# Who sums the weights of the down product, and when: accumulating transfers, VectorE and tile order in a decoder layer

## The chip, the cores and the metric

The kernel is one launch on one core of a Trainium2 chip. A core has TensorE (matrix products), VectorE, ScalarE and GpSimd (called PE, DVE, ACT and POOL in the profile) and SyncE (SP), which here only issues DMA transfers. Transfers issued by SP and by POOL go to the core's 16 DMA engines. A transfer issued by POOL can also add what it brings to what is at its destination (an accumulating transfer). Each engine works through its own instructions in order. The metric is the time of one execution in microseconds on the device; lower is better.

## The reference

One decoder layer on 512 tokens of width 1024, in float32: a gated linear recurrence and a sparse attention side by side, merged, and then a gated MLP with a short convolution. What bears on the change is the MLP's end:

```python
up = causal_dwconv(rms_norm(x, norm2_g) @ w_up, ffn_conv_w, ffn_conv_b)
gate, val = jnp.split(up, 2, axis=-1)
x = x + (jax.nn.gelu(gate) * val) @ w_down
```

`w_up` is 1024 x 6144 and `w_down` is 3072 x 1024.

## The kernel before

**Products.** A float32 product is made from three products of split operands: high times high, high times low, low times high (`mm3`, and `mm` in `down`, lines 1526 to 1528). So each weight tile is loaded raw, cast to a high part by ScalarE (`whi`, line 200), and VectorE or GpSimd subtracts to get the low part (`wlo`, lines 208 and 205).

**Strassen's scheme.** Most of the up product and all of the down product use the Strassen-Winograd form: a 2 x 2 block product from seven products instead of eight, for sums and differences of the blocks. The sums of weight blocks are needed as weight tiles of their own. For the up product and for part of the down product they are made in DRAM, long before they are needed: `sums` (lines 1254 to 1296) copies blocks to a DRAM tile (`ws6` to `ws23` for the up product, `dn0` to `dn11` for the down product) and adds others by accumulating transfers of POOL (line 1268). It has 83 steps. `_wprep` calls one or more of them as it prepares the weight tiles, whose order is `PLAN` (229 tiles; up product from index 97, the Strassen part from 109, down product from 181). `SUM_AT` is the index at which the first step is issued, `SUM_RATE` how far apart in tiles the next ones are, by index.

**The down product** (`down`, lines 1512 to 1621) has twelve tiles n of the inner dimension, each from two chunks of 128 rows. Phase one runs n = 0 to 11 with four of the seven products (tiles `d1` and `d2`, 1024 columns each), for four quarters p of the output columns, 48 matmuls for each n. Then `mix` combines the PSUM banks of each quarter with one copy on ScalarE and four additions on VectorE. Phase two runs n = 0 to 11 again with the other three products (`d3`, 1024 columns, and `d4`, 512), 36 matmuls for each n. `down_ops` and `down_ops2` make the activations' operands (`dt`, `dh`, `dl`) on VectorE and ScalarE.

**The loads.** `down_load(m)`, m = 0 to 23 over both phases, loads two raw tiles: `dg` and `ds`, from three slots each. In phase one `ds` becomes `d2`: its left half is a block of the weights, to which a second block has to be added; the right half comes from a DRAM sum. `dg` becomes `d1`: one block and another DRAM sum. Where n is odd or below 3, POOL adds the second block to `ds` by an accumulating transfer (line 1317). Elsewhere VectorE does, from `dg` (line 1333). In phase two the left half of `d3` is a DRAM sum plus one more block. For odd n that block is added in DRAM by an accumulating transfer in the load of phase one (line 1322). For even n VectorE adds it (line 1331).

**What sets the order.** On TensorE the order is as written. On the other engines a planner orders the instructions by its own cost estimates, by the order of the program and by priorities; `issue_after` puts an instruction behind a named one. `w` prepares weight tiles two ahead (`WLEAD`), and at the first tile of each n `_wprep` calls `down_load` two loads ahead and `down_sums` one tile ahead:

```python
if name in ("d1", "d3") and m:
    self.down_load(m + 2)
    self.down_sums(m + 1)
```

Phase two begins with tile 0 for quarters 0 to 2, then tile 1 for quarter 0, then tile 0 for quarter 3.

## Time and profile before

| what | value |
|---|---|
| median of 3 runs | 1040.7 us (1034.25 to 1041.61) |
| profiled execution | 1032.89 us |
| its span, first to last instruction | 1031.0 us |
| TensorE busy | 1006.5 us (98%) |
| VectorE busy | 810.3 us (79%) |
| ScalarE busy | 645.9 us (63%) |
| GpSimd busy | 275.1 us (27%) |
| moved by DMA | 186.66 MB, mean 181 GB/s |

The span is shorter than the execution, since it runs from the first to the last instruction. Busy time of TensorE is modelled and includes the pipelining of matmuls, so 98% doesn't mean that TensorE works at its peak in that time. A row of the timeline has the start and the length in us, the engine, the line, the operation and its tiles; in brackets stands how long the engine was idle before it and what ended the idle time. In the windows view each engine has its busy time and its number of instructions; then come the granted TensorE clock, the mean busy share of the 16 DMA engines and the GB/s they moved.

### The profile page before, as it was taken

To read this page: it belongs to the slowest core of one execution; us is meant where nothing else is said; L and a number is where in the kernel's file an instruction comes from. 1 tells how busy PE (TensorE), PEld (TensorE's weight loads), DVE (VectorE), ACT (ScalarE), POOL (GpSimd) and SP (SyncE) were. 2 spreads that over 40 slices of the span, in tenths; PEclk is the share of its full clock that TensorE was granted. 3 is DMA by queue.
4 is the path that set the end of the run, shared out by engine and by line. 5 is a ranking of instruction groups with operands and counts; after the bars stand their busy time and mean duration, and the time that the engine had idled before them with its cause. 6 is when DMAs were issued, how large, how long until landed. Compare 5 with 4: busy or idle time off the path is not lost.

```text
span 1031.0 us, 16984 instructions
## 1 busy us (share of the span) xinstructions
PE 1006.5 (98%) x6089; PEld 893.5 (87%) x6089; DVE 810.3 (79%) x1565; ACT 645.9 (63%) x1076; POOL 275.1 (27%) x353
## 2 busy tenths in 40 slices
PE   9998999999999999999999999999999999988998
PEld 7897888988888878888888888888999999987998
DVE  6778878889878778779598464599888888987876
ACT  6466776877777654488788543465566666654453
POOL 0166435335443320241332114222111111310000
PEclk9999999999999999999999999999999999999999
DMA  6537756677657797564534987655656566776553
GB/s 233 117 108 202 220 144 158 168 180 170 189 139 195 193 285 235 156 182 122 155 102 117 301 240 219 171 159 170 191 186 195 184 184 201 221 193 183 155 184 134
DMA packets 75365, 186.66 MB, mean 181 GB/s; under 512 B 18059, under 2 KB 19723, under 8 KB 71440
## 3 DMA queue, kind: packets, MB, share of 16 engines
q1 hardware_dynamic: 66064, 153.65, 45.6%
q0 software_dynamic: 9072, 31.77, 17.8%
q8 instruction: 48, 0.79, 0.3%
q14 instruction: 37, 0.30, 0.1%
q10 hardware_dynamic: 144, 0.15, 0.1%
HBM read 176.32 MB, written 58.20 MB: 227 GB/s over the span
## 4 chain that ended last, share of the span: by engine, by line
PE 71%; DVE 11%; DMA 10%; issue 3%; ACT 3%; POOL 1%; SPq 1%; DVEq 0%; ACTq 0%; POOLq 0%
PE mm L239 11%; PE mm L238 11%; PE mm L237 11%; PE mm L1417 6%; PE mm L1415 6%; PE mm L1416 6%; PE O L947 4%; DVE wlo L208 3%; PE T L956 3%; DMA wraw<-in_w 2%; PE mm L1527 2%; PE mm L1526 2%; PE mm L1528 2%; PE S L916 1%; PE S L917 1%
## 5 line engine op out<-in xcount | busy, mean ns | idle before, releaser
L200 ACT CAST whi<-wraw 128x1024 fp32r<-128x1024 f32 (+3 forms) x178 | 177.8, 999 | 135.5 <-PE mm L1416 56.4
L208 DVE TENSOR_TENSOR wlo<-wraw,whi 128x1024 fp32r<-128x1024 f32 (+2 forms) x145 | 166.2, 1146 | 56.3 <-ACT whi L200 56.2
L237 PE MATMUL mm<-xh,whi 128*128 128x512 f32 x456 | 178.7, 392 | 0.0
L239 PE MATMUL mm<-xh,wlo 128*128 128x512 f32 x456 | 178.5, 391 | 0.0
L238 PE MATMUL mm<-xl,whi 128*128 128x512 f32 x456 | 178.2, 391 | 0.0
L205 POOL TENSOR_TENSOR wlo<-wraw,whi 128x256 fp32r<-128x256 f32 (+1 forms) x131 | 96.8, 843 | 74.5 <-ACT whi L200 69.9
L239 PEld LDWEIGHTS mm<-xh,wlo 128*128 128x128 f32 x456 | 85.6, 188 | 18.4
L237 PEld LDWEIGHTS mm<-xh,whi 128*128 128x128 f32 x456 | 85.7, 188 | 16.9
L238 PEld LDWEIGHTS mm<-xl,whi 128*128 128x128 f32 x456 | 85.6, 188 | 16.9
L927 ACT ACTIVATE s<-s,bs,rq 128x128 f32<-128x128 f32 (+3 forms) x128 | 82.5, 647 | 19.1 <-DVE bs L924 19.0
L1528 PE MATMUL mm<-dh,wlo 128*128 128x256 f32 x300 | 85.1, 284 | 5.1 <-DVE wlo L208 5.1
L1527 PE MATMUL mm<-dl,whi 128*128 128x256 f32 x300 | 84.7, 282 | 3.8 <-DVE dl L263 3.8
L1526 PE MATMUL mm<-dh,whi 128*128 128x256 f32 x300 | 84.8, 283 | 0.1
L263 DVE TENSOR_TENSOR ptl<-T,pth 128x512 fp32r<-128x512 f32 x80 | 55.0, 688 | 17.3 <-ACT pth L262 16.4
L1268 POOL DMA_DIRECT2D ws<-ws x36 | 28.3, 786 | 136.0 <-DMA ws<-in_wa 68.7
L262 ACT CAST pth<-T 128x512 fp32r<-128x512 f32 x80 | 46.4, 583 | 27.2 <-PE T L956 26.5
L1528 PEld LDWEIGHTS mm<-dh,wlo 128*128 128x128 f32 x300 | 57.1, 190 | 6.4 <-DVE wlo L208 6.4
L1527 PEld LDWEIGHTS mm<-dl,whi 128*128 128x128 f32 x300 | 57.0, 190 | 4.5 <-DVE dl L263 4.5
L920 DVE CUSTOM_DVE_ANT_0 s<-S,cc 128x128 f32<-128x128 f32 (+3 forms) x128 | 57.9, 482 | 1.5 <-PE S L917 1.1
L1526 PEld LDWEIGHTS mm<-dh,whi 128*128 128x128 f32 x300 | 56.9, 190 | 0.6 <-DVE mm L1558 0.3
L956 PE MATMUL T<-cc,s 128*128 128x128 f32 x320 | 48.4, 273 | 2.7 <-DVE s L932 1.3
L956 PEld LDWEIGHTS T<-cc,s 128*128 128x128 f32 x320 | 39.3, 140 | 12.8 <-DVE s L932 1.8
(439 smaller groups left out, 2872.5 us busy)
## 6 DMA issues: line engine op xcount, KB each, us to landing
wraw<-in_w SPq DMA_DIRECT2D x102, 512.0 KB, 3.6
ws<-in_wi SPq DMA_DIRECT2D x36, 512.0 KB, 5.6
wraw<-ws SPq DMA_DIRECT2D x72, 256.0 KB, 3.1
wraw<-in_w SPq DMA_DIRECT2D x54, 256.0 KB, 3.2
ws<-in_wa POOLq DMA_DIRECT2D x18, 512.0 KB, 7.5
ws<-ws POOLq DMA_DIRECT2D x36, 256.0 KB, 4.6
dn<-in_wd SPq DMA_DIRECT2D x12, 512.0 KB, 5.2
ds<-in_w SPq DMA_DIRECT2D x24, 256.0 KB, 3.6
```

Of the source, the lines that this page charges most:

```text
L200: self.last_hi = nc.scalar.copy(hi[:, :n], raw[:, :n])
L205: nc.gpsimd.tensor_sub(lo[:, e], raw[:, e], hi[:, e].bitcast(F32))
L208: nc.vector.tensor_sub(lo[:, :e], raw[:, :e], hi[:, :e].bitcast(F32))
L237: nc.tensor.matmul(ps, wh, xh, start=first, stop=False)
L238: nc.tensor.matmul(ps, wh, xl, start=False, stop=False)
L239: nc.tensor.matmul(ps, wl, xh, start=False, stop=last)
L927: self.last_exp = nc.scalar.activation(s[t, x], s[t, x], AF.Exp, bias=bs[:, x, t:t + 1], scale=rq[:, t], accum_out=sm[:, x, t:t + 1])
L956: nc.tensor.transpose(T[:, off:off + 128], s[i, x][:, 128 * j:128 * j + 128], self.ident)
L1415: nc.tensor.matmul(ps, w[0][:, c], xh, start=start and k == 0, stop=False, skip_group_check=True)
L1526: nc.tensor.matmul(ps, w[0][:, c], x[0][:, i], start=start, stop=False, skip_group_check=True)
L1527: nc.tensor.matmul(ps, w[0][:, c], x[1][:, i], start=False, stop=False, skip_group_check=True)
L1528: nc.tensor.matmul(ps, w[1][:, c], x[0][:, i], start=False, stop=stop, skip_group_check=True)
```

## The change

Five things are changed together.

1. Which sums are made by whom. The tiles of `ACC1` (0, 1, 2, 5, 8, 11) have the second block of `ds` added by an accumulating transfer, and those of `ACC2` (0, 1, 2, 5, 8) the DRAM sum of phase two; VectorE makes the other six and seven sums.
2. When VectorE sums. `down_sums` is called for the tile that is being prepared, not for the next, and issued behind the last `wlo` on VectorE (`last_lo`).
3. The DRAM accumulate of phase two is issued two loads later than before.
4. Phase two takes the half tile first: `d4` stands before `d3` in the plan, the product that uses it (`c`) comes first for each quarter, and the order of tiles and quarters is the plain one from n = 0.
5. `SUM_AT` and `SUM_RATE` have other values: the first step of `sums` is issued at index 20, not 17, and the steps are spaced differently.

```diff
-SUM_AT, SUM_RATE = 17, ((43, 0.55), (54, 1.5), (80, 5.0), (116, 1.4), (999, 2.4))
+SUM_AT, SUM_RATE = 20, ((43, 0.65), (54, 2.0), (80, 4.0), (116, 1.2), (999, 2.4))
 WLEAD = 2
+ACC1, ACC2 = (0, 1, 2, 5, 8, 11), (0, 1, 2, 5, 8)
...
     for n in range(FC // 2):
-        p += [("d3", n, 1024), ("d4", n, 512)]
+        p += [("d4", n, 512), ("d3", n, 1024)]
...
-            m = c + FC // 2 * (name == "d3")
-            if name in ("d1", "d3") and m:
+            m = c + FC // 2 * (name == "d4")
+            if name in ("d1", "d4") and m:
                 self.down_load(m + 2)
-                self.down_sums(m + 1)
+                with self.tc.issue_after(self.last_lo.ins):
+                    self.down_sums(m)
...
-                nc.vector.tensor_sub(lo[:, :e], raw[:, :e], hi[:, :e].bitcast(F32))
+                self.last_lo = nc.vector.tensor_sub(lo[:, :e], raw[:, :e], hi[:, :e].bitcast(F32))
...
             if late:
-                dma(g[:, 512:], w[i, :, 512:1024])
+                dma(g[:, 512:], w[WIDX[("d3", n)], :, 512:1024])
                 dma(g[:, 0:512], self.dsum(n, 1))
-                dma(s[:, 0:512], w[i + 1, :, 0:512])
+                dma(s[:, 0:512], w[WIDX[("d4", n)], :, 0:512])
+                self.dn_raw[("d3", n)], self.dn_raw[("d4", n)] = g, s
             else:
+                i = WIDX[("d1", n)]
                 dma(s[:, 0:512], w[i, :, 512:1024])
-                if n % 2 or n < 3:
-                    self.nc.gpsimd.dma_start(s[:, 0:512], w[i, :, 0:512], accum_op=ALU.add)
+                if n in ACC1:
+                    q(s[:, 0:512], w[i, :, 0:512], accum_op=ALU.add)
                 dma(g[:, 0:512], w[i, :, 0:512])
                 dma(g[:, 512:], self.dsum(n, 1))
                 dma(s[:, 512:], self.dsum(n, 0))
-                if n % 2:
-                    self.nc.gpsimd.dma_start(self.dsum(n, 1), w[WIDX[("d3", n)], :, 512:], accum_op=ALU.add)
...
+        if m - 2 in ACC2:
+            q(self.dsum(m - 2, 1), w[WIDX[("d3", m - 2)], :, 512:], accum_op=ALU.add)
...
-        if late < 2 and n % 2 == 0 and (late or n > 2):
-            g, s = (self.dn_raw[(k, n)] for k in (("d3", "d4") if late else ("d1", "d2")))
-            if late:
-                self.nc.vector.tensor_tensor(g[:, 0:512], g[:, 0:512], g[:, 512:], ALU.add)
-            else:
-                self.nc.vector.tensor_tensor(s[:, 0:512], s[:, 0:512], g[:, 0:512], ALU.add)
+        if late and n not in ACC2:
+            g = self.dn_raw[("d3", n)]
+            self.nc.vector.tensor_tensor(g[:, 0:512], g[:, 0:512], g[:, 512:], ALU.add)
+        elif not late and n not in ACC1:
+            g, s = self.dn_raw[("d1", n)], self.dn_raw[("d2", n)]
+            self.nc.vector.tensor_tensor(s[:, 0:512], s[:, 0:512], g[:, 0:512], ALU.add)
...
-            W[n] = self.w("d3", n, WLEAD), self.w("d4", n, WLEAD)
-
-        def two(p, n, which="dac"):
+            w4 = self.w("d4", n, WLEAD)
+            W[n] = self.w("d3", n, WLEAD), w4
+
+        def two(p, n, which="cda"):
...
-        get2(0)
-        for p in range(3):
-            two(p, 0)
-        get2(1)
-        for p, n in ((0, 1), (3, 0), (1, 1), (2, 1), (3, 1)):
-            two(p, n)
-        for n in range(2, N - 2):
+        for n in range(N - 2):
             get2(n)
             for p in range(4):
                 two(p, n)
```

The calls of `down_sums(0)` and `down_sums(1)` ahead of the loop are taken out as well; they did nothing for these tiles.

More of the change, by code (lines that the diff above doesn't have):

```diff
@@ L1307, in down_load @@
             s = self.dtile(m, [128, 1024], F32, "ds", ("b11l", "t3l"))
-            i = WIDX[("d3" if late else "d1", n)]
-            w, dma = self.a["w"], self.nc.sync.dma_start
+            w, dma, q = self.a["w"], self.nc.sync.dma_start, self.nc.gpsimd.dma_start
             if late:
-                dma(g[:, 512:], w[i, :, 512:1024])
+                dma(g[:, 512:], w[WIDX[("d3", n)], :, 512:1024])
                 dma(g[:, 0:512], self.dsum(n, 1))
-                dma(s[:, 0:512], w[i + 1, :, 0:512])
+                dma(s[:, 0:512], w[WIDX[("d4", n)], :, 0:512])
+                self.dn_raw[("d3", n)], self.dn_raw[("d4", n)] = g, s
             else:
+                i = WIDX[("d1", n)]
                 dma(s[:, 0:512], w[i, :, 512:1024])
-                if n % 2 or n < 3:
-                    self.nc.gpsimd.dma_start(s[:, 0:512], w[i, :, 0:512], accum_op=ALU.add)
+                if n in ACC1:
+                    q(s[:, 0:512], w[i, :, 0:512], accum_op=ALU.add)
                 dma(g[:, 0:512], w[i, :, 0:512])
@@ L1320, in down_load @@
                 dma(s[:, 512:], self.dsum(n, 0))
-                if n % 2:
-                    self.nc.gpsimd.dma_start(self.dsum(n, 1), w[WIDX[("d3", n)], :, 512:], accum_op=ALU.add)
-            self.dn_raw[PLAN[i][:2]], self.dn_raw[PLAN[i + 1][:2]] = g, s
+                self.dn_raw[("d1", n)], self.dn_raw[("d2", n)] = g, s
+        if m - 2 in ACC2:
+            q(self.dsum(m - 2, 1), w[WIDX[("d3", m - 2)], :, 512:], accum_op=ALU.add)
     def down_sums(self, m):
         n, late = m % (FC // 2), m // (FC // 2)
-        if late < 2 and n % 2 == 0 and (late or n > 2):
-            g, s = (self.dn_raw[(k, n)] for k in (("d3", "d4") if late else ("d1", "d2")))
-            if late:
-                self.nc.vector.tensor_tensor(g[:, 0:512], g[:, 0:512], g[:, 512:], ALU.add)
-            else:
-                self.nc.vector.tensor_tensor(s[:, 0:512], s[:, 0:512], g[:, 0:512], ALU.add)
+        if late and n not in ACC2:
[4 more added lines that the diff above has]
+            self.nc.vector.tensor_tensor(s[:, 0:512], s[:, 0:512], g[:, 0:512], ALU.add)
     def ffn(self):
@@ L1474, in ffn @@
                     fd.tile([128, 56], F32, name="fdpad")
-                elif j == FC - 2:
-                    self.down_sums(0)
                 elif nx is None:
@@ L1519, in down @@
         self.down_load(2)
-        self.down_sums(1)
         X = {0: first, 1: self.down_ops(1, fs)}
```

## The prediction

> **What bounds the kernel now.** I read the busy time by stretches first, to find where the span still has room, then the order of the matmuls, then the chain of waits, and last the order on VectorE and the DMA issues.
>
> ```profile
> span 1031.0 us, 16984 instructions
> core 0: us, PE busy (x) PEld busy (x) DVE busy (x) ACT busy (x) POOL busy (x), PEclk, DMA share, GB/s
> 840.00:880.00 40.00, 40.00 (x345) 40.00 (x344) 33.69 (x49) 25.77 (x35) 5.21 (x4) 1.00 0.62 191
> 880.00:920.00 40.00, 37.23 (x310) 36.42 (x309) 35.71 (x52) 23.81 (x32) 10.65 (x9) 1.00 0.81 217
> 920.00:960.00 40.00, 34.42 (x272) 33.62 (x273) 30.40 (x55) 19.07 (x25) 5.17 (x6) 0.96 0.72 189
> ```
>
> In the windows view (PE is the first pair of columns) TensorE is the bound: 40.00 of 40 us in the gated product's steady state. A gain can only come from stretches like the last two, 2.8 and 5.6 us short. They hold the down product, lines 1526 to 1528.
>
> ```profile
> L1526 PE MATMUL mm<-dh,whi 128*128 128x256 f32 x300 | 84.8, 283 | 0.1
> ...
> L1526 PE MATMUL misc<-dh,whi 128*128 128x256 f32 x36 | 10.3, 286 | 0.8 <-DVE misc L1558 0.8
> ```
>
> ```profile
> 893.53 0.28 PE L1526 MATMUL mm<-dh,whi 128*128 128x256 f32 x1
> ...
> 1023.83 0.28 PE L1526 MATMUL mm<-dh,whi 128*128 128x256 f32 x1
> ...
> 1026.17 0.28 PE L1528 MATMUL mm<-dh,wlo 128*128 128x256 f32 x1
> ```
>
> Two groups of the lines view give 300 + 36 matmuls to each of the three lines, 1,008 in all (48 per tile n in phase one, 36 in phase two). In the order of time the first starts at 893.53 and the last at 1026.17. Undisturbed, the last 21 start 2.34 us apart over 20 steps, 0.117 us each. So 1,007 steps need 117.8 us and take 132.6: **the down product loses 14.8 us**, which caps what mending this stage can bring. At this pace a tile lasts 48 x 0.117 = 5.6 us in phase one and 4.2 in phase two. The named waits, in brackets:
>
> ```profile
> 907.67 0.38 PE L1527 MATMUL mm<-dl,whi 128*128 128x256 f32 x1 [1.84 <-DVE dl L263]
> ...
> 920.77 0.38 PE L1527 MATMUL mm<-dl,whi 128*128 128x256 f32 x1 [1.53 <-DVE dl L263]
> ...
> 933.34 0.39 PE L1528 MATMUL mm<-dh,wlo 128*128 128x256 f32 x1 [0.98 <-DVE wlo L208]
> ...
> 948.74 0.39 PE L1528 MATMUL mm<-dh,wlo 128*128 128x256 f32 x1 [3.50 <-DVE wlo L208]
> ...
> 977.82 0.39 PE L1526 MATMUL misc<-dh,whi 128*128 128x256 f32 x1 [0.77 <-DVE misc L1558]
> ...
> 979.74 0.38 PE L1527 MATMUL mm<-dl,whi 128*128 128x256 f32 x1 [0.48 <-DVE dl L263]
> ```
>
> The first four come at n = 2, 4, 6 and 8 (1.84 + 1.53 + 0.98 + 3.50 = 7.85 us), always for a `wlo` or `dl` of VectorE; the last two (1.25) follow the mix between the phases. The chain of waits says why VectorE is late:
>
> ```profile
> 908.21 2.28 DVE wlo L208 x2
> 910.51 0.33 SPq L1315
> 910.94 6.81 DMA ds<-dn
> 917.76 2.35 DVE wlo L208 x2
> 920.11 0.61 DVE dl L263
> ```
>
> It is a ring: `wlo` frees the raw tile, SP issues the next load (0.33 us), the load lands 6.8 us later, and only then does VectorE go on to the next `wlo`. What holds VectorE to the load is seen in its own order:
>
> ```profile
> 903.71 0.69 DVE L1333 TENSOR_TENSOR ds<-ds,dg 128x512 f32<-128x512 f32 x1 [1.11 <-DMA ds<-in_w]
> ...
> 917.15 0.69 DVE L1333 TENSOR_TENSOR ds<-ds,dg 128x512 f32<-128x512 f32 x1 [3.18 <-DMA ds<-in_w]
> 917.76 1.22 DVE L208 TENSOR_TENSOR wlo<-dg,whi 128x1024 fp32r<-128x1024 f32 x1
> ...
> 920.03 0.68 DVE L263 TENSOR_TENSOR dl<-fxh,dh 128x512 fp32r<-128x512 f32 x1
> 920.63 0.42 DVE L1495 SCALAR_TENSOR_TENSOR fxh<-dt,fxh 128x256 f32<-128x256 f32 x1
> ...
> 931.46 0.69 DVE L1333 TENSOR_TENSOR ds<-ds,dg 128x512 f32<-128x512 f32 x1 [3.05 <-DMA ds<-in_w]
> ...
> 946.86 0.69 DVE L1333 TENSOR_TENSOR ds<-ds,dg 128x512 f32<-128x512 f32 x1 [3.73 <-DMA ds<-in_w]
> ...
> 960.14 0.69 DVE L1331 TENSOR_TENSOR dg<-dg 128x512 f32<-128x512 f32 x1 [2.95 <-DMA dg<-dn]
> ...
> 969.45 0.69 DVE L1331 TENSOR_TENSOR dg<-dg 128x512 f32<-128x512 f32 x1 [1.60 <-DMA dg<-dn]
> ```
>
> The lines 1333 and 1331 are the sums. Counting the `wlo` of `dg`, that of 917.76 belongs to tile 4, but the sum ahead of it, at 917.15, is tile 6's. Likewise those of 903.71, 931.46 and 946.86 are for tiles 4, 8 and 10, each put ahead of the `wlo` of a tile two earlier. VectorE stood idle 1.11, 3.18, 3.05 and 3.73 us for loads not needed for two more tiles, with a `wlo` that TensorE needed at once behind them. Lines 1331 do it again (2.95 and 1.60 us) before the mix.
>
> **The change part by part.** *Tying the sum to tile order.* Each sum now belongs to its own tile m and is issued behind the `wlo` of tile m - 1, so it moves back past two tiles. Removed are the four named waits, 7.85 us, and what hangs on them. The wait of 3.50 us is followed by a lower granted clock:
>
> ```profile
> 950.00:955.00 5.00, 5.00 (x30) 5.00 (x31) 5.00 (x10) 0.00 (x0) 1.19 (x2) 0.66 0.74 211
> ```
>
> At 0.66 these 5 us lose 5 x 0.34 = 1.7 us. That leaves 14.8 - 7.85 - 1.25 - 1.7 = 4.0 us, restarts (the matmul after a wait is 0.38 us long, not 0.28) and waits too short for a long bracket. I share it by the named waits: 7.85/9.1 of 4.0 = 3.4 us, so phase one holds 7.85 + 1.7 + 3.4 = 13.0 us.
>
> The Trainium skill ("TensorE: Matmul & The Clock Gate", section "Part 1: The HAM clock gate") says that the array falls to half clock after an idle window of about 3.4 us. The trace agrees (after 3.50 us yes, after 1.84 no). By that rule the 1.7 us go with the wait; had the clock fallen for another reason, the sum below would be 1.7 us less, 9.8.
>
> What stays: at n = 2 VectorE still has the gated product's last work behind it. It loses the wait of 1.11 and the early sum of 0.61 us, 1.72 against TensorE's 1.84 plus a restart, and tile 3's new sum (0.61) is near: 0.4 to 1.0 us stay, I take 0.7. Gain: 13.0 - 0.7 = 12.3 us.
>
> *What the tied sum adds.* Behind it wait ScalarE's `whi` of the second half, that tile's `wlo`, and TensorE. Is its load there? There are three raw slots, so load n + 1 is issued after the `wlo` of tile n - 2, that is during tile n - 3 and about 3.5 us into it (two casts and two `wlo`), and the cast wants it 1 us into tile n: 3 x 5.6 - 2.5 = 14.3 us. The prices:
>
> ```profile
> ds<-dn SPq DMA_DIRECT2D x9, 256.0 KB, 4.4
> dn<-in_w POOLq DMA_DIRECT2D x5, 256.0 KB, 5.0
> ds<-in_w POOLq DMA_DIRECT2D x5, 256.0 KB, 6.8
> ```
>
> A plain load needs 0.33 + 4.4, at the worst row 0.33 + 6.8 = 7.1 us, and leaves 7 us. With an accumulating transfer behind it (tiles 5, 8, 11) it is 0.33 + 4.4 + 6.8 = 11.5 and leaves 2.8. So I cost the wait at nothing. Without that cover it is one for one on TensorE.
>
> *Which engine sums.* In phase one six tiles are summed by VectorE instead of four, in phase two seven instead of six: three more at 0.61 us from start to start (917.15 to 917.76) is 1.8 us of VectorE, and three fewer transfers of 5.0 to 6.8 us. VectorE's phase-one tile is two `wlo` (917.76 to 920.03, 2.27), two `dl` (0.60 each, 920.03 to 920.63) and three small operations of at most 0.42: 4.7 us, 5.3 with a sum, under TensorE's 5.6. So it costs 0 (bounds: 0 and 1.8). Delaying the DRAM accumulate by two loads takes it out of the moment when its own tile's load is read: POOL issues it later, the reader is a phase away, cost 0. POOL's queue only holds the other accumulating transfers there.
>
> *Half tile first.* In phase two the 512-column `d4` needs half the cast and subtraction, so TensorE can start earlier. But with the reordering removed, tile 0 of quarter 3 comes after 27 matmuls (3.2 us) instead of 36 (4.2), nearer to its mix. The named waits there are 1.25 us, and VectorE arrives earlier by the gone wait and sum at 969.45 (1.60 + 0.61) against 1.05 us of lost lead. Bounds: 1.25 gained, 2.0 lost; as a gone wait need not shift the mix in full, I take the middle, 0.4 lost.
>
> *Respreading the DRAM sums.* The same 83 steps are issued, starting three weight tiles later and ending 20 later, so fewer in the heads and more in the recurrent stage, the merge and the first gated tiles. In the heads a sum's transfer sits on the chain once:
>
> ```profile
> 164.71 5.31 DMA ws<-in_wa
> ```
>
> ```profile
> 176.00 0.63 PE L956 MATMUL T<-cc,s 128*128 128x128 f32 x4 [1.31 <-DVE ptl L263]
> ```
>
> POOL stood behind it 5.3 us, and TensorE then waited 1.31. Such a wait can go or appear elsewhere: 1.3 gained to 1.3 lost. I take 0.4 lost, a third of one such wait, since the steps now reach over more stages. The far ends are rivals below.
>
> Sum: 12.3 - 0.4 - 0.4 = **11.5 us**, span 1031.0 to 1019.5. The profiled execution took 1032.9 us (1.9 around its span), 7.8 under the median of the three runs and below their lowest. Nothing in the page shows what the slower runs add, so I carry the gain over whole: 1040.7 - 11.5 = 1029.2 us.
>
> **The rivals.** *The wait moves to the load.* If the stage's DMA delays grow, tiles 5, 8 and 11, whose lead leaves 2.8 us, are late. For it: once TensorE doesn't stop, the same bytes come in 12 us less, and the DMA share is already 0.81 in the stretch from 880. Against: three fewer accumulates. Three waits of 1.5 and a slow quarter 3 (2.0) give back 6.5: a gain of 5, 1036 us.
>
> *The respread sums hit the gated product's start.* Thirteen of the steps, 70 to 82, now fall on weights 109 to 130, some 54 us at four weights per 9.8 us (84 matmuls); before, two did. By the tiles' sizes they carry 5.7 MB more, 106 GB/s on the 191 of that stage at share 0.62, where full would be 191/0.62 = 308. Issued evenly it just fits. But weights 109 to 116 are fetched together as buffers come free, and hold seven steps, 3.7 MB, 12 us of full DMA. If all this reached TensorE, the gain would be gone: 1041 us. Against: weights are loaded up to four tiles ahead. The Trainium skill ("Trainium Kernel Development and Optimization", section "Key Constraints") says that transfers from all queues run on the same 16 DMA engines and interleave, which is this mechanism; no row of this run shows it at that place.
>
> *Slower: POOL stands in the recurrent stage.* There POOL's queue also prepares the convolution's tile, and steps 39 to 47 now fall there, three steps of three dependent accumulates.
>
> ```profile
> POOL ws L1268 <- DMA ws<-in_wa: 68.7, 13, 7.9
> ...
> POOL ws L1268 <- DMA ws<-in_wi: 61.9, 13, 12.1
> ...
> POOL ws L1268 <- DMA ws<-ws: 36.8, 12, 5.5
> ```
>
> ```profile
> 456.46 46.86 SPq L194 DMA_DIRECT2D wraw<-in_w  x10
> ```
>
> The longest POOL waits for such a step add to 7.9 + 12.1 + 5.5 = 25.5 us. A weight tile there takes 46.86/10 = 4.7 us, and I take the lead of a convolved tile over its gate as two, 9.4. Two steps at the longest would stop TensorE 2 x 16.1 = 32 us: 1040.7 - 11.5 + 32 = 1061. It decides once a step holds POOL over 9.4 us. Against: steps four weights apart find their sources landed, and mean waits (5.3 + 4.8 + 3.1) give only 13.2.
>
> *It doesn't do what it says.* If VectorE's order still puts a sum ahead of an earlier `wlo`, the ring stays: 1040 us.
>
> **How the numbers follow.** Forecast 0.64, load late 0.14, gated start 0.11, POOL 0.07, order unchanged 0.04. The forecast's own range is a gain of 8 to 15 (the whole 14.8 back, or phase one's less 4): 1026 to 1033. One per cent, about what a measurement tells from no change, is 10.4 us; I put 0.52 of the forecast's 0.64 beyond it. Faster 0.52, within 1% 0.41 (0.12 + 0.14 + 0.11 + 0.04), slower 0.07. The range: the runs' offset may not carry over, so below it reaches to 1021.4, the profiled time less the gain; above to 1040, which takes in the late load.
>
> **What would show it.** Right: lines 1333 and 1331 without idle time ahead of them, each between the `wlo` of tiles n - 1 and n; the waits at n = 4, 6 and 8 gone; the granted clock 1.00 in the stage; first to last matmul of the down product near 121 us. Wrong: ScalarE waiting for `ds` loads, waits at quarter 3 after the mix, or TensorE idle between 400 and 720 us.

## The result and the profile after

The changed kernel takes 1025.8 us (median of 4 runs, 1025.06 to 1027.07), the kernel before 1041.15 (4 runs, 1034.25 to 1041.69). The ratio is 0.987, with a 95% interval of 0.983 to 0.991. The forecast was 1029.2 us, a ratio of 0.989. One execution of one kernel below (the even sums) took 1418.93 us at a mean granted clock of 0.654, where all others have 0.987 or more; it is left out everywhere.

The two profiled executions differ by far less than the medians: 1032.89 against 1027.07 us, 5.8 us. So the table cuts both spans into stretches by the first matmul of the next stage: the recurrence and attention heads up to the first matmul of the attention output; from there to the first matmul of the up product's Strassen part; that part up to the last matmul of `t4h` with a high part ("gated"); and the down product from its first to its last matmul. Two matmuls (0.35 us) lie between the last two, and 4.9 us before, 5.2 after, behind the last.

| stretch (us) | before | after | difference |
|---|---|---|---|
| heads | 368.0 | 364.0 | -4.0 |
| up to the Strassen part | 349.1 | 348.6 | -0.5 |
| gated product's Strassen part | 176.1 | 185.0 | +8.9 |
| down product | 132.6 | 122.1 | -10.5 |

**The down product** is what the prediction worked on. In the windows view of the kernel after, TensorE's column (the first pair) and the granted clock (third from the right) answer the rows shown of before:

```profile
core 0: us, PE busy (x) PEld busy (x) DVE busy (x) ACT busy (x) POOL busy (x), PEclk, DMA share, GB/s
700.00:710.00 10.00, 10.00 (x46) 8.29 (x45) 9.86 (x15) 5.86 (x8) 4.83 (x4) 1.00 1.01 307
710.00:720.00 10.00, 10.00 (x77) 9.53 (x76) 9.40 (x17) 6.09 (x8) 6.47 (x6) 1.00 0.96 247
720.00:730.00 10.00, 10.00 (x88) 10.00 (x87) 4.61 (x8) 2.26 (x3) 1.57 (x2) 1.00 1.07 318
730.00:740.00 10.00, 8.50 (x57) 8.08 (x56) 7.65 (x11) 6.09 (x8) 2.79 (x3) 0.83 0.81 258
740.00:750.00 10.00, 10.00 (x88) 10.00 (x88) 9.10 (x13) 6.27 (x9) 1.69 (x3) 1.00 1.02 302
750.00:760.00 10.00, 6.34 (x48) 6.14 (x47) 4.61 (x8) 3.94 (x5) 2.05 (x2) 0.89 0.62 139
...
880.00:920.00 40.00, 38.36 (x322) 37.58 (x321) 38.90 (x58) 26.42 (x35) 10.76 (x9) 1.00 0.79 214
920.00:960.00 40.00, 40.00 (x345) 40.00 (x344) 38.00 (x64) 21.71 (x29) 2.56 (x3) 1.00 0.68 205
950.00:955.00 5.00, 5.00 (x45) 5.00 (x44) 4.69 (x7) 3.04 (x4) 0.00 (x0) 1.00 0.84 254
```

From 920 to 960 TensorE is busy for all 40 us (34.42 before) at clock 1.00. The stretch from 950, where the clock stood at 0.66 before, has 1.00 too. VectorE's sums, by the lines view from 895 to 1022 (`dg` are those of phase two, `ds` those of phase one; the last column is the idle time ahead of them, which before was 4.9 and 11.1 us, all for loads):

```profile
L1333 DVE TENSOR_TENSOR dg<-dg 128x512 f32<-128x512 f32 x7 | 4.8, 684 | 0.0
L1336 DVE TENSOR_TENSOR ds<-ds,dg 128x512 f32<-128x512 f32 x6 | 4.1, 690 | 0.0
```

And the order on TensorE, from the first to the last matmul of the down product, with all the waits of over half a microsecond that are left:

```profile
897.94 0.28 PE L1526 MATMUL mm<-dh,whi 128*128 128x256 f32 x1
...
910.81 0.39 PE L1527 MATMUL mm<-dl,whi 128*128 128x256 f32 x1 [0.85 <-DVE dl L265]
...
912.55 0.39 PE L1527 MATMUL mm<-dl,whi 128*128 128x256 f32 x1 [0.76 <-DVE dl L265]
...
972.84 0.38 PE L1526 MATMUL mm<-dh,whi 128*128 128x256 f32 x1 [1.48 <-DVE mm L1558]
...
1020.08 0.28 PE L1528 MATMUL mm<-dh,wlo 128*128 128x256 f32 x1
```

Two waits stay at n = 2 and one after the mix at quarter 3. Those of n = 4, 6 and 8 are gone.

**The gated product** is where time came back that the forecast didn't have. The windows from 700 to 760 show why one should look there: the DMA share is 0.96 to 1.07 up to 750, apart from 730 to 740 (0.81); in these windows before it was 0.60 to 0.68. In 730 to 740 and 750 to 760 TensorE loses 1.50 and 3.66 us and some of its clock. The timeline of the kernel after, all engines in order of time, names the waits:

```profile
730.66 1.05 ACT L202 CAST whi<-wraw 128x1024 fp32r<-128x1024 f32 x1 [5.53 <-DMA wraw<-ws]
...
731.76 0.39 PE L1418 MATMUL mm<-t1h,whi 128*128 128x256 f32 x1 [0.76 <-ACT whi L202]
...
733.01 0.39 PE L1420 MATMUL mm<-t1h,wlo 128*128 128x256 f32 x1 [0.75 <-DVE wlo L210]
...
746.95 0.80 POOL L1270 DMA_DIRECT2D dn<-dn  x1 [6.86 <-DMA dn<-in_we]
...
753.94 0.76 POOL L1270 DMA_DIRECT2D dn<-dn  x1 [5.39 <-DMA dn<-in_we]
754.47 1.52 POOL L1361 TENSOR_TENSOR f<-y 128x512 f32<-128x512 f32 x1
756.02 0.42 DVE L1495 TENSOR_TENSOR dt<-f 128x256 f32<-128x256 f32 x1 [5.35 <-POOL f L1361]
...
756.83 1.22 DVE L210 TENSOR_TENSOR wlo<-wraw,whi 128x1024 fp32r<-128x1024 f32 x1
...
758.10 0.58 PE L1420 MATMUL mm<-t1h,wlo 128*128 128x256 f32 x1 [3.65 <-DVE wlo L210]
```

There are two chains. At 730 a weight tile lands late, while the DMA engines are full, and ScalarE waits 5.53 us for it. At 746 to 756 POOL stands 6.86 and 5.39 us for one accumulating transfer before it may issue the next, which builds on it, and the multiplication of gate and value (line 1361) is queued behind it. VectorE's `dt` waits 5.35 us for that product, and the `wlo` that TensorE needs is queued behind `dt`. So a transfer for a product that starts 143 us later stopped TensorE for 3.65 us, through two engines that keep their order. Behind each chain the granted clock is at 0.50 for 3.41 us (733.84 to 737.25 and 757.73 to 761.14 by the windows view), 1.7 us lost each time. So the first chain costs 0.76 + 0.75 + 1.7 = 3.2 us and the second 3.65 + 1.7 = 5.35, together 8.6 of the 8.9, if the clock's fall is put down to the waits.

### The profile page after: what moved, and what is told of

Same layout as the page of the kernel before. It is cut to its first block, busy times and chain, and to the rows that moved or that the text cites. A ratio compares the mean times of both kernels' runs of the same rounds, so it can differ in the third digit from the quotient of the medians.

```text
span 1025.3 us, 16991 instructions
## 1 busy us (share of the span) xinstructions
PE 1005.7 (98%) x6089; PEld 895.6 (87%) x6089; DVE 807.7 (79%) x1569; ACT 645.8 (63%) x1075; POOL 273.8 (27%) x350
## 5 line engine op out<-in xcount | busy, mean ns | idle before, releaser
L240 PE MATMUL mm<-xl,whi 128*128 128x512 f32 x456 | 178.3, 391 | 0.0
```

What stands on the lines that cost most here:

```text
L240: nc.tensor.matmul(ps, wh, xl, start=False, stop=False)
```

## The experiments

Three questions were open. Which part of the change gives the gain? What did the respread sums do, where the forecast had only 0.4 us? And where does the difference between the medians (15 us) and the profiles (5.8 us) come from? Each kernel's stretches:

| kernel | heads | up to Strassen | gated | down | median us (runs) | ratio to before, 95% |
|---|---|---|---|---|---|---|
| before | 368.0 | 349.1 | 176.1 | 132.6 | 1041.15 (4) | |
| after | 364.0 | 348.6 | 185.0 | 122.1 | 1025.8 (4) | 0.987 (0.983 to 0.991) |
| before, again | 370.1 | 347.8 | 176.1 | 131.5 | 1040.33 (10) | 0.999 (0.996 to 1.002) |
| down product's part alone | 370.1 | 354.2 | 176.1 | 122.0 | 1028.94 (4) | 0.990 (0.984 to 0.996) |
| respread alone | 365.1 | 348.2 | 184.9 | 129.7 | 1038.09 (10) | 1.000 (0.997 to 1.003) |
| sums over early | 365.2 | 352.9 | 176.1 | 122.8 | 1024.0 (4) | 0.986 (0.981 to 0.990) |
| tie alone | 369.1 | 349.9 | 176.1 | 125.0 | 1030.15 (10) | 0.993 (0.990 to 0.997) |
| after without the tie | 365.3 | 348.3 | 183.6 | 129.1 | 1034.11 (8) | 0.996 (0.992 to 0.999) |
| gate on VectorE | 363.5 | 348.0 | 178.3 | 122.2 | 1021.27 (2) | 0.986 (0.979 to 0.992) |
| even sums | 364.4 | 352.4 | 176.1 | 123.8 | 1019.17 (6) | 0.982 (0.979 to 0.986) |
| even sums, gate on VectorE | 363.4 | 351.6 | 176.3 | 122.7 | 1020.36 (6) | 0.982 (0.979 to 0.986) |
| even sums, old order of phase two | 362.8 | 352.8 | 176.3 | 121.5 | 1018.27 (6) | 0.981 (0.977 to 0.984) |
| before, a longer execution | 372.8 | 353.8 | 176.1 | 135.6 | 1045.25 (1) | |

The stretches are of one profiled execution each, the medians of all runs. Runs of before beside these had medians of 1039.76, 1038.71 and 1038.99 us on three chips. The 83 steps of `sums`, counted from `SUM_AT` and `SUM_RATE`, fall on the weight indices so:

| values | below 54 | 54 to 79 | 80 to 108 | from 109 (Strassen part) |
|---|---|---|---|---|
| before | 55 | 6 | 20 | 2 |
| after | 41 | 7 | 22 | 13 |
| over early | 41 | 20 | 22 | 0 |
| even | 41 | 13 | 28 | 1 |

**The kernel before, once more**, unchanged, for the size of a difference that means nothing.

> The kernel before, unchanged, for a second profile of it. Its usual runs took some 8 us more than its profiled one (1041 against 1032.9). Theory A: the extra lies in the ring of late sums, so a profile near 1041 has the down product at 140 us or more from first to last matmul, not 132.6. Theory B: it lies in the heads, so the attention output's matmuls begin near 376 us, not 368.

Measured: 1040.33 us over 10 runs, from 1032.47 to 1042.57; the ratio to the other runs of before is 0.999 (0.996 to 1.002). Single executions of before spread over 10 us, and the profiled one was again the shortest. So one execution of before isn't a fair base for one of after. As the profile is again that of a short run, it can't tell the two theories apart.

**The down product's part alone**: the changed kernel with the old spread of the sums.

```diff
-SUM_AT, SUM_RATE = 20, ((43, 0.65), (54, 2.0), (80, 4.0), (116, 1.2), (999, 2.4))
+SUM_AT, SUM_RATE = 17, ((43, 0.55), (54, 1.5), (80, 5.0), (116, 1.4), (999, 2.4))
```

> The whole change but for SUM_AT and SUM_RATE, which are those of before. My theory: the down product takes 122 us from first to last matmul as in the changed kernel, and the gated product's Strassen part is back at 176.5 us from its first to its last matmul (changed kernel: 185.3). By theory A all that the usual runs gain is here or more: 1024 to 1026 us. By theory B 1029 to 1031 us.

Measured: down product 122.0 us, gated product back at 176.1, median 1028.94 us (theory B's, within 0.1 us), ratio 0.990 (0.984 to 0.996). So the gain of the down product comes without the respread, and the loss of the gated product is the respread's alone. The profiled execution loses 5.1 us against before in the stretch up to the Strassen part. On TensorE, in the attention output (a third wait, of 1.25 us, is at 410.05):

```profile
387.31 0.50 PE L239 MATMUL mm<-oh,whi 128*128 128x512 f32 x1 [0.70 <-ACT whi L202]
...
390.54 0.50 PE L241 MATMUL mm<-oh,wlo 128*128 128x512 f32 x1 [2.49 <-DVE wlo L210]
```

**The respread alone**: before with the new values.

```diff
-SUM_AT, SUM_RATE = 17, ((43, 0.55), (54, 1.5), (80, 5.0), (116, 1.4), (999, 2.4))
+SUM_AT, SUM_RATE = 20, ((43, 0.65), (54, 2.0), (80, 4.0), (116, 1.2), (999, 2.4))
```

> The kernel before with the new SUM_AT and SUM_RATE alone. My theory: the heads are over some 4 us earlier and the gated product's Strassen part takes 185 us instead of 176.5, so by theory A about 1044 us; by theory B, where the heads' usual loss goes with the thinner transfers, about 1036 us. The down product keeps its ring, 132 us or more.

Measured: the gated product takes 184.9 us, as in after, and the heads 365.1, as in after. On TensorE the gated product's wait is even longer here than after's 3.65:

```profile
756.75 0.58 PE L1417 MATMUL mm<-t1h,wlo 128*128 128x256 f32 x1 [5.25 <-DVE wlo L208]
```

It is the second chain alone: POOL stands 6.52 us for `dn<-in_we` (up to 752.59), `dt` waits 6.58 us for its product (754.68), and the clock is at 0.50 from 754.39 to 761.20. The wait and the 3.4 us of clock are 8.65 of the 8.8 us lost.

The time is no different from before: 1.000 (0.997 to 1.003), between what the two theories gave (1036 and 1044 us). Against the means of the five profiles with the old values, the heads are 4.9 us shorter, and the down product's 129.7 us lie below the 131.5 to 135.6 of the three profiles of before. Together they make up for the gated product.

**The sums over early**: the changed kernel with no step on the Strassen part.

```diff
-SUM_AT, SUM_RATE = 20, ((43, 0.65), (54, 2.0), (80, 4.0), (116, 1.2), (999, 2.4))
+SUM_AT, SUM_RATE = 20, ((43, 0.65), (54, 2.0), (116, 1.3), (999, 2.4))
```

> The changed kernel with its thin start of the DRAM sums, but one step every 1.3 weights from index 54 on, so that the last one is issued at index 107, ahead of the gated product's Strassen part. My theory: that part is back at 176.5 us and nothing else changes, 1025.8 - 8.8 = 1017 us. Rival: POOL, held by the accumulates, or the fuller DMA engines stop TensorE in the recurrent stage or the merge, 1022 us or more, with waits of TensorE between 400 and 650 us.

Measured: the gated product is back at 176.1 us, all 8.9 us of it, and the heads keep their gain (365.2). But 4.3 us appear ahead of the Strassen part, where 20 steps now lie in place of 7 (indices 54 to 79), so the 1017 us of the theory are missed and its rival has come. In the timeline, in the recurrent stage:

```profile
503.43 0.70 PE L1112 MATMUL mm<-st,whi 126*128 126x512 f32 x2 [3.05 <-DMA st<-xcl]
```

and the windows view of the same kernel:

```profile
490.00:500.00 10.00, 10.00 (x46) 8.26 (x44) 7.79 (x9) 7.41 (x11) 5.01 (x10) 1.00 0.96 258
500.00:510.00 10.00, 6.95 (x24) 5.26 (x23) 2.47 (x4) 6.04 (x8) 2.65 (x4) 0.83 0.82 234
```

The DMA engines are at 0.96 there, and the convolved tile `st`, which POOL's queue brings, lands late: `st<-xch` takes 4.7 us from issue to landing in the middle, against 2.9 in after. POOL also stood 5.33 and 3.98 us for sums at 480 and 486, with other transfers of that stage queued behind; whether that had a part in the wait isn't shown. The net is 1024.0 us, 0.986 (0.981 to 0.990), which can't be told from after.

**The tie alone**: before, with the sum of its own tile behind the last `wlo`, and nothing else.

```diff
-                self.down_sums(m + 1)
+                with self.tc.issue_after(self.last_lo.ins):
+                    self.down_sums(m)
...
-                nc.vector.tensor_sub(lo[:, :e], raw[:, :e], hi[:, :e].bitcast(F32))
+                self.last_lo = nc.vector.tensor_sub(lo[:, :e], raw[:, :e], hi[:, :e].bitcast(F32))
```

> The kernel before with one thing changed: each sum on VectorE is made for its own tile and behind the last wlo. Which sums are made by whom, the order of phase two and the DRAM sums are as before. My theory: the late sums are the whole of it, so the down product takes 122 to 124 us from first to last matmul, and the time is 1028 to 1031 us. Rival: the fewer and later accumulating transfers are what made the loads land in time, so the down product stays at 128 us or more.

Measured: down product 125.0 us, 7.6 less than before (6.5 to 10.6 less than its three profiles) and 1 more than the theory's upper end, ratio 0.993 (0.990 to 0.997). The one long wait that it leaves is at n = 2, here with what stands ahead of it:

```profile
902.10 0.96 POOL L1318 DMA_DIRECT2D ds<-in_w  x1
...
909.17 1.04 ACT L201 CAST whi<-ds 128x1024 fp32r<-128x1024 f32 x1 [1.70 <-issue]
...
910.25 1.22 DVE L209 TENSOR_TENSOR wlo<-ds,whi 128x1024 fp32r<-128x1024 f32 x1 [1.14 <-ACT whi L201]
...
912.13 0.38 PE L1528 MATMUL mm<-dl,whi 128*128 128x256 f32 x1 [3.13 <-DVE dl L264]
```

The first row is the accumulating transfer for tile 3's `ds`. It takes 7.0 us to land, at 909.1; ScalarE's cast of that tile starts 0.1 us later, after 1.70 us of idle time for which the profile names no cause. VectorE's `wlo` waits for the cast, and the `dl` of n = 2 is queued behind it. The clock is then at 0.50 from 912.5 to 915.9, another 1.7 us. In the changed kernel VectorE sums tile 3.

**After without the tie**: the new choice of tiles and the new order of phase two, but the sum one tile early and put where the planner likes.

```diff
-                with self.tc.issue_after(self.last_lo.ins):
-                    self.down_sums(m)
+                self.down_sums(m + 1)
```

> The changed kernel without the tie: its sums are called one tile ahead and placed by the planner, as before; all else is as in the changed kernel. My theory: the ring is back, VectorE waits over 1 us for loads ahead of several sums, and the down product takes 128 us or more (1033 us in all). Rival: with three transfers fewer the loads land in time, 122 to 124 us.

Measured: 129.1 us for the down product, 1034.11 in all. The idle time ahead of VectorE's sums is back. The lines view from 895 to 1022 of this kernel (the sums are lines 1332 and 1335 here):

```profile
L1332 DVE TENSOR_TENSOR dg<-dg 128x512 f32<-128x512 f32 x7 | 4.8, 688 | 2.9 <-DMA dg<-dn 2.9
L1335 DVE TENSOR_TENSOR ds<-ds,dg 128x512 f32<-128x512 f32 x6 | 4.1, 689 | 7.1 <-DMA ds<-in_w 7.1
```

With the same six and seven sums in the changed kernel, both columns read 0.0. So it is the tie, not the choice of tiles, that frees VectorE: 129.1 to 122.1 with it, 132.6 to 125.0 by it alone. The rest of the part, that is the choice of tiles, the later DRAM accumulate and the half tile together, makes the 3.0 us between the tie alone (125.0) and the down product's part (122.0). Without the tie it makes 0.6 us with the same spread of the sums (respread alone, 129.7, to 129.1).

The gated product's second chain is in this kernel too: POOL stands 6.63 us for a transfer, `dt` waits 5.30 for its product, and TensorE 2.87 at 757.65.

**Gate on VectorE**: the changed kernel, with the multiplication of gate and value moved from POOL to VectorE for the six chunks around the start of the Strassen part. If the second chain above holds, the wait of 3.65 us goes though the same sums are issued at the same place. If the full DMA alone did it, it stays.

```diff
-            (nc.vector if j == FC - 1 else nc.gpsimd).tensor_mul(fs(j), yg, yv)
+            (nc.vector if j == FC - 1 or NPL - 2 <= j < NPL + 4 else nc.gpsimd).tensor_mul(fs(j), yg, yv)
```

> The changed kernel with the gating multiplication of chunks 4 to 9 on VectorE instead of POOL, so that it doesn't stand behind POOL's accumulating transfers. If POOL's order is what stops the gated product, the wait of 3.65 us at 758 goes, and the Strassen part takes 179 to 181 us instead of 185.0; the two waits near 732, where ScalarE waited for loads, stay. If it is the fullness of the DMA engines alone, it stays at 184 us or more.

Measured: gated product 178.3 us, so 6.7 of the 8.9 are back. What is left on TensorE:

```profile
730.90 0.38 PE L1420 MATMUL mm<-t1h,wlo 128*128 128x256 f32 x1 [0.76 <-DVE wlo L210]
...
739.15 0.39 PE L1420 MATMUL mm<-b11h,wlo 128*128 128x256 f32 x1 [0.98 <-DVE wlo L210]
```

POOL stands 6.03 and 6.62 us for its transfers here too (up to 742.98 and 751.17), the DMA share is 0.84 to 1.08 from 700 to 760, and TensorE doesn't stop for either. So the larger part of the loss came by POOL's order and not by the full DMA engines alone: 5.35 us by the rows of after, and up to 6.7 by this kernel. The difference is mainly the clock, which stays at 1.00 here from 700 to 765, also behind the first wait. Ahead of that wait ScalarE again waits 4.21 us for a weight. Ahead of the second VectorE has no idle time over 0.2 us from 732.24 on, with the moved multiplication in its row, so how much of the 2.2 us left is due to late weights isn't shown. The two runs took 1019.45 and 1023.1 us, 0.986 (0.979 to 0.992).

**Even sums**: the changed kernel with the steps spread more evenly ahead of the Strassen part (13 and 28 at the two middle places, one behind).

```diff
-SUM_AT, SUM_RATE = 20, ((43, 0.65), (54, 2.0), (80, 4.0), (116, 1.2), (999, 2.4))
+SUM_AT, SUM_RATE = 20, ((43, 0.65), (54, 2.0), (80, 2.0), (116, 1.0), (999, 2.4))
```

> The changed kernel with its thin start of the DRAM sums, one step per 2.0 weights from index 43 to 80 (thinner in the recurrent stage than the 1.3 that stopped TensorE for 3.05 us there) and one per weight from 80 on, the last at index 108. My theory: neither the recurrent stage nor the gated product stops, 1017 to 1019 us. Rival: the merge and the output product, with a step for every weight, now lose what the recurrent stage gains, 1022 us or more.

Measured: 1019.43, 1019.27 and 1019.75 us, 0.984 (0.979 to 0.989). A second run is for a profile:

> The kernel with the evenly spread DRAM sums again, for an undisturbed profile. My theory: the Strassen part of the gated product takes 176.1 us, the way from the attention output to its first matmul 348 to 349 us, and 1019 to 1020 us in all.

Measured: 1019.17 us, 0.982 (0.979 to 0.986). The gated product is at 176.1 us, and the wait for `st` that the sums over early had is gone. But the stretch up to the Strassen part takes 352.4 us, not the 348 to 349 expected. Most of that is in the attention output:

```profile
378.17 0.50 PE L241 MATMUL mm<-oh,wlo 128*128 128x512 f32 x1 [2.28 <-DVE wlo L210]
```

This wait can't come of the edit: up to 430 us after and all three kernels with even sums run the same instructions in the same order on every engine, and after has 0.42 us there. Without the attention output's matmuls the stretch takes 304.9 us, against 304.5 in after.

**Even sums and gate on VectorE** together, both edits on the changed kernel:

```diff
-SUM_AT, SUM_RATE = 20, ((43, 0.65), (54, 2.0), (80, 4.0), (116, 1.2), (999, 2.4))
+SUM_AT, SUM_RATE = 20, ((43, 0.65), (54, 2.0), (80, 2.0), (116, 1.0), (999, 2.4))
...
-            (nc.vector if j == FC - 1 else nc.gpsimd).tensor_mul(fs(j), yg, yv)
+            (nc.vector if j == FC - 1 or NPL - 2 <= j < NPL + 4 else nc.gpsimd).tensor_mul(fs(j), yg, yv)
```

> The same with the gating multiplication of chunks 4 to 9 on VectorE as well. My theory: with no sums left in the gated product POOL holds nothing there, so the second remedy adds nothing: within 0.5 us of the kernel without it. Rival: POOL's accumulates ahead of the Strassen part also held the gating, and it gains 1 us or more.

Measured: 1020.36 us, 0.982 (0.979 to 0.986), which can't be told from the even sums alone (1019.17); the gated product takes 176.3 us. Once the sums are out of the Strassen part, POOL has nothing to stand behind, and moving its work buys nothing. That fits the cause named for the gated product.

**Even sums and the old order of phase two**: `d3` before `d4`, and tile 1 for quarter 0 between quarters 2 and 3 of tile 0, as before the change, on the even sums.

```diff
-        p += [("d4", n, 512), ("d3", n, 1024)]
+        p += [("d3", n, 1024), ("d4", n, 512)]
...
-            m = c + FC // 2 * (name == "d4")
-            if name in ("d1", "d4") and m:
+            m = c + FC // 2 * (name == "d3")
+            if name in ("d1", "d3") and m:
...
-        def two(p, n, which="cda"):
+        def two(p, n, which="dac"):
...
-        for n in range(N - 2):
+        get2(0)
+        for p in range(3):
+            two(p, 0)
+        get2(1)
+        for p, n in ((0, 1), (3, 0), (1, 1), (2, 1), (3, 1)):
+            two(p, n)
+        for n in range(2, N - 2):
```

> The kernel with the evenly spread sums, with phase two in the order of before: d3 before d4, product d first, tile 0 of quarter 3 after tile 1 of quarter 0. This measures the half tile by itself. My theory: the wait of 1.5 us at quarter 3 after the mix goes and the two of before (0.8 and 0.5) come in its place, so the down product takes 122 us again, within 0.5 us. Rival: the half tile's earlier start is worth 1 us or more, and this kernel is so much slower.

Measured: the down product takes 121.5 us, the shortest of all, and on TensorE nothing over half a microsecond is left after the mix; the two waits at n = 2 are the only ones (the two of before that were expected back didn't come):

```profile
905.15 0.39 PE L1527 MATMUL mm<-dl,whi 128*128 128x256 f32 x1 [0.85 <-DVE dl L265]
...
906.89 0.38 PE L1527 MATMUL mm<-dl,whi 128*128 128x256 f32 x1 [0.77 <-DVE dl L265]
```

The wait of 1.48 us after the mix belongs to the new order, which takes quarter 3 after 27 matmuls: all seven profiles with that order have 1.47 or 1.48 us there, and the two with the tie and the old order 0.47 (the tie alone) and none over 0.4 (this one). In the whole time the 0.9 us to the even sums (1018.27 against 1019.17) lie within the scatter. This is the fastest kernel found, 0.981 (0.977 to 0.984). The three kernels with even sums lie at 1014.88 to 1024.03 us in 21 runs, after at 1025.06 to 1027.07 in 4.

**A longer execution of before**, for its profile: the first two profiles of before were its shortest runs.

> The kernel before once more, for a profile of one of its usual runs (1036 to 1043 us; the two profiled so far took 1032.9 and 1032.5). If it is one, the stage times show where the extra lies: the attention output and what is ahead of it (368 to 370 us to its first matmul, 348 to 349 us from there to the gated product), or the down product (131.5 to 132.6 us).

Measured: 1045.25 us, 12.4 more than in the first profile. The gated product is the same (176.1). It loses 4.8 us in the heads, 4.7 up to the Strassen part and 3.0 in the down product. On TensorE, its long waits in the heads and the attention output, where the first profile has one of 1.67 us from 200 to 420:

```profile
225.86 1.12 PE L956 MATMUL T<-cc,s 128*128 128x128 f32 x4 [1.48 <-DVE ptl L263]
...
359.74 0.66 PE L956 MATMUL T<-cc,s 128*128 128x128 f32 x4 [1.49 <-DVE ptl L263]
...
391.59 0.50 PE L237 MATMUL mm<-oh,whi 128*128 128x512 f32 x1 [2.26 <-ACT whi L200]
...
393.54 0.80 PE L239 MATMUL mm<-oh,wlo 128*128 128x512 f32 x1 [1.21 <-DVE wlo L208]
```

and the windows view of it, with the clock that goes with them:

```profile
360.00:400.00 40.00, 36.53 (x158) 29.61 (x157) 27.02 (x35) 18.46 (x29) 6.75 (x9) 0.91 0.82 243
...
920.00:925.00 5.00, 5.00 (x37) 5.00 (x37) 3.64 (x9) 1.70 (x3) 1.60 (x2) 0.80 0.95 234
```

So this longer run of before loses in the stages in which most sums are issued and in the ring of the down product. The DMA share alone doesn't tell the two runs apart: it is 0.82 from 360 to 400 here and 0.86 in the first profile. Over half of the difference is clock: it is at 0.50 for 3.41 us behind the wait at 225.86, for 6.83 from 392.94 on and for 3.41 from 918.59 on, 6.8 us lost in all, at places where the first profile has 1.00. The other executions of before say the same: of 60, the 14 under 1036 us have a mean granted clock of 0.995 and the 19 over 1041 us one of 0.990, which is 4.7 of the 9.4 us between them. That answers the third question in part. Stages that the change relieves were also where before's runs scatter, so its first profile showed too little of what there was to gain.

## Why the prediction was right, and where it wasn't

*The bound and the ring.* Right. The forecast saw that a sum put ahead of an earlier `wlo` makes VectorE stand for a load. Taking only that order away gave 7.6 us, and putting only that order back cost 7.0.

*Phase one: 13.0 us less 0.7 at n = 2.* Right in kind, and a little too much. The waits of 1.53, 0.98 and 3.50 us are gone, and the clock's 1.7 us with the last. What was mis-sized is the rest at n = 2: 0.7 was put there, and two waits of 0.85 and 0.76 stay (1.61). The reason given, VectorE behind the gated product's work, is what these rows show: both end on a `dl` of VectorE with no idle time of VectorE around it.

*Which engine sums: 0.* The tied sums cost no wait, as costed (idle 0.0 ahead of all thirteen, no wait on TensorE in phase one after n = 2). The choice of tiles, the later DRAM accumulate and the half tile together were worth a further 3.0 us beside the tie, though; the prediction put the first two at nothing and the third at 0.4 lost. With the tie alone, waits of 0.85 and 3.13 us stay at n = 2, and 1.7 us of clock behind them; the down product's part has 0.82 and 0.77 there and no lower clock. The rows of the tie alone lead the 3.13 us back to tile 3's own accumulating transfer, which landed 7.0 us after its issue; after the change VectorE sums that tile. POOL's queue there holds not only accumulating transfers, as the prediction had it: ahead of this one stands a multiplication of 3.28 us (from 898.08). Against that stands the wait after the mix (1.48 against 0.47). The edits weren't tested one by one.

*The lead of the loads.* Right: none of the thirteen sums had idle time ahead of it. The rival of the late load fell with that.

*Half tile first: 0.4 lost.* Right in sign, too small in size, and inside its bounds. The prediction set the new order's wait against the 1.25 us of before. But with the tie and the old order those are 0.47 us or gone, so the 1.48 us are nearly all the new order's. With the old order the down product takes 121.5 us, 0.5 to 1.3 less than in five other kernels with the full down part (122.0 to 122.8); the sixth, the even sums at 123.8, has 1.7 us of lower clock at n = 2. The part behind the last matmul is 0.3 us longer in all kernels with the new order (5.2 against 4.9 us). The half tile buys nothing here that a run can show.

*The sum for the stage.* 132.6 - 12.3 + 0.4 = 120.7 was forecast, 122.1 measured. Of the 1.4 us, 0.9 are the waits at n = 2.

*Respreading the sums: 0.4 lost, between 1.3 lost and 1.3 gained.* **This is the step that failed.** In the profiles it lost 8.9 us in the gated product and won 4.0 in the heads. Both are outside the bounds, and so is their sum, 4.9 us lost. The heads' gain was seen as one wait of 1.31 us at most. Over all profiles the heads take 368.0 to 372.8 us with the old values (five profiles) and 362.8 to 365.3 with the new ones or those derived from them (eight profiles), 5.8 us between the means. The gated product's loss was in the prediction as a rival, "the respread sums hit the gated product's start", at 0.11 and up to 12 us. It came true at three quarters of that price, and the DMA share of 1.01 to 1.07 is the full DMA that it worked out from 191 GB/s at 0.62. The 308 GB/s estimated for a full share were measured as 302 to 318 in the three full windows of after.

What the rival had wrong is the way to TensorE. It thought of weights that land late, and by the rows of after that gave 3.2 us with its clock. The larger part, 5.35 us, came by POOL, whose multiplication stood behind accumulating transfers; the respread alone lost its 8.8 us by that chain only. The prediction did have POOL's order as a rival, but in the recurrent stage. The place could have been read from the kernel before: its gated product multiplies on POOL in every chunk but the last, and thirteen steps were to fall there.

The Trainium skill ("Trainium Kernel Development and Optimization", section "Key Constraints") says that transfers of all queues run on the same 16 DMA engines and interleave. The rows at 730 agree: ScalarE waits 5.53 us for a weight of SP's queue while POOL's sums run. The larger chain needs the order of one engine besides: with the gate on VectorE the transfers are as full and as slow, and it is gone.

*POOL stands in the recurrent stage.* Not in after: TensorE has no such wait there, with 7 steps in place of 6 at the indices 54 to 79. With 20 steps there a wait appeared. It ends on a late transfer of the same queue, and the stretch lost 4.3 us where the rival had 32.

*The offset of the runs, carried over whole.* **This failed too**, in the other direction. The median lies 3.4 us below the forecast although the respread cost 4.9 us between the two profiles (8.9 less 4.0), not 0.4. Before's median lay 8.3 us above its profiled execution, after's 1.3 below its own. The longer run of before shows where such time can sit: 4.8 us in the heads, 4.7 in the attention output and what follows, 3.0 in the ring, over half of it lower clock. The change thins out the sums in the first two and removes the third. So the range's lower end, 1021.4, which assumed that the offset doesn't carry over, was the better thought about the runs. By the profiles the forecast was 5.7 us too fast (1032.9 - 11.5 = 1021.4 against 1027.07), by the medians 3.4 too slow. That the median came so close is in part luck, since the two errors partly cancel.

*Cancelling parts, in medians.* Old values and old down product took 1040.3 us, the respread alone 1038.1, the down part alone 1028.9, both 1025.8 (this one beside other runs of before than the first three). The down part is worth 11.4 to 12.3 us, which is the forecast's 11.9 (12.3 less 0.4 for the half tile). In the profiles its stage gained 10.5, so this agreement too contains what scatters between runs. The respread's 2.2 to 3.1 can't be told from nothing (1.000, 0.997 to 1.003).

*What stays open.* The three profiles of the even sums have 351.6 to 352.8 us ahead of the Strassen part, against 348.6 in after. In two the difference is the attention output (47.5 and 47.1 us from its first to its last matmul, against 44.1), where they run the same instructions as after, so it is scatter between runs. In the third it is a stretch near 610 us with three short waits and 1.7 us of lower clock; whether that belongs to the even sums, one profile can't say. Open is also which edit beside the tie makes the 3.0 us, and why the clock falls behind some waits and not behind others.

## What to carry to other kernels

Before moving background work in time, list for each engine that issues it what else stands in its queue at the new place, and follow that one engine further. A step that waits for its own earlier transfer holds all that is queued behind it. A load-dependent instruction that is wanted late should be tied to the place where it is wanted, since an engine that keeps its order pays the load's whole delay. Compare stages over several executions before carrying a gain onto a median, because the stages that a change relieves may be those in which the runs scatter.

## What the runs showed of the hardware

**The granted clock falls after less idle time than the prediction took.** It took 3.50 us as enough and 1.84 as not. In the stretches right behind, over 4 to 5 us, the windows show: 0.66 after one wait of 2.28 us (even sums, 378 to 383), 0.66 after 0.70 and 2.49 us within 4 us (down part alone, 390 to 395), 0.73 after 0.76 and 0.75 us within 2 us (after, 732 to 736) and 0.66 after 0.22, 0.52 and 0.58 us within 3 us. The last, in the even sums with the old order:

```profile
606.22 0.50 PE L240 MATMUL mm<-ml,whi 128*128 128x512 f32 x1 [0.22 <-DVE ml L265]
...
607.47 0.51 PE L239 MATMUL mm<-mh,whi 128*128 128x512 f32 x1 [0.52 <-ACT mh L264]
...
608.56 0.50 PE L240 MATMUL mm<-ml,whi 128*128 128x512 f32 x1 [0.58 <-DVE ml L265]
```

```profile
609.00:614.00 5.00, 5.00 (x17) 3.93 (x16) 2.58 (x3) 2.19 (x3) 1.54 (x2) 0.66 0.89 226
614.00:619.00 5.00, 5.00 (x24) 4.14 (x23) 2.40 (x3) 2.20 (x3) 0.00 (x0) 1.00 0.85 254
```

But it doesn't always fall: 0.85 and 0.76 us within 2 us at n = 2 in after were followed by 1.00, the 0.82 and 0.77 at the same place in the even sums by 0.66 (907.9 to 912.9); the wait of 1.84 in before by 1.00, that of 1.83 in its longer execution by 0.66 (918.6 to 923.6). Between 100 and 1010 us each drop in these traces lasts 3.41 us at 0.50, in two cases twice that. So a short wait can cost its own length and 1.7 us of clock besides, or not, from run to run. The Trainium skill ("TensorE: Matmul & The Clock Gate", section "Part 1: The HAM clock gate") gives an idle window of about 3.4 us and says that the window is free-running and that results vary between runs. The varying agrees, but 3.4 us of unbroken idle time isn't needed by these rows. That each such drop is caused by the waits in front of it was not tested apart.

**Accumulating transfers in a full stretch are slow for the engine that waits on them.** POOL stood 6.86 and 5.39 us for two of 256 KB (`dn<-in_we`, up to 747 and 754). They took 9.0 and 6.2 us from issue to landing, where the DMA share was 0.92 and 0.94; in before, where these transfers are issued earlier, the twelve of them have a median of 4.4 us.
